# One projection chunk of 512 columns for sparse attention's key and two heads' memory queries

## The chip, the cores and the metric

The kernel runs on one core of a Trainium2 chip. A core has five engines with queues of their own: TensorE (PE, with its weight loads shown apart as PEld), VectorE (DVE), ScalarE (ACT), GpSimd (POOL) and SyncE (SP), which here only issues transfers. The metric is the time of one execution on the device in microseconds (us). The time before is the median of three runs.

## What is computed

Two layers of a decoder trunk over 512 tokens of width 1024. In each layer the normed input `h` is projected by one wide matrix `w_in`, whose column groups feed four branches; each branch is lifted back to 1024, gated, summed, and followed by an output projection and a feed-forward part. The change touches two of these column groups:

```python
h = rmsnorm(x, norm_mix)
(a_x, a_b, a_c, d_q, d_k, d_v, i_q, i_k, i_w,
 g_q, g_f, g_i, g_g, m_q, gate_logits) = split_cols(h @ w_in)
...
k = partial_rope(rmsnorm(d_k.reshape(b, s, 1, 64), dsa_k_norm), cos, sin)[:, :, 0]
...
mq = rmsnorm(m_q.reshape(b, s, 4, 128), mem_q_norm)
ml = jnp.einsum('bshd,bmhd->bhsm', mq, mk) * (128 ** -0.5)
mp = jax.nn.softmax(ml, axis=-1)
y_m = jnp.einsum('bhsm,bmhd->bshd', mp, mv)
```

The first is the key chunk of the sparse attention, 256 columns: key (64), value (64) and the first two of eight index heads (128). The second is the query of the memory attention, four heads of 128 columns, each normed over its own 128 columns, against 256 memory tokens.

## The kernel before

**Layout.** `h` is held feature-major: 8 chunks of 128 features, each 128 partitions x 512 tokens, split into a high and a low part of type fp32r. Every product is three matmuls, high x high, high x low, low x high (`mm3`, lines 316, 317 and 319, where nearly all matmuls of the profile have their line). The norm of `h` is not applied to `h` itself: its reciprocal `r_t` (one number a token, tokens on the partitions) or `r_b` (the same as a row, copied to all partitions) is multiplied in when a product is read out of PSUM.

**Weight chunks.** `wchunk` loads a column group of a weight matrix in parts of 128 x 1024 numbers (tiles `w_raw`, four buffers, issued by SyncE, line 220), and splits each part: ScalarE makes `w_hi` (line 101, the helper for all activations), VectorE `w_lo` (line 245), three buffers each. A 256-column group over 8 feature chunks is two parts of four chunks; a 512-column group is four parts of two.

**Two ways to use a chunk.** `features` makes a feature-major product: the weights are the stationary operand, 512 tokens of `h` move through, one PSUM bank for 128 columns. `tokens` and `tokens_wide` make a token-major one: 128 tokens of `h` are stationary and the weight columns move, so a matmul is as wide as the column group, and there are four products, one for each tile of 128 tokens. `tokens_wide` goes through the parts in the outer loop and needs all four banks at once; with `in_turn` a part's matmuls wait in order for the part before.

**PSUM.** Eight banks of 128 x 512: three `mm` (projections), three `tr` (transposes, norm sums, and a fourth bank for wide products), two `at` (attention).

**The stages around the change.** In `mixer`, four generators run in turn by a script of letters, `EARLY`: `m` is the memory attention (`mem_branch`), `b` the sparse attention's projections, `c` the short convolution, `s` the selection of keys, `n` the late fetch of `r_b`. Each letter runs a generator to its next `yield`; the order so written is the priority by which a planner, with a simulated timeline, orders each engine's queue. Parts inside `tc.high_priority` go ahead of it; `add_manual_dep` fixes an order of two instructions by hand.

**Memory queries before.** For heads 0 and 1 (`q == 0`) and for 2 and 3, `mem_branch` loads a 256-column chunk, makes two feature-major products with `features`, and reads each product out three times: scaled into `qg_hi`, squared into `sq`, and the remainder into `qg_lo` (line 759). The head's mean square per token comes from TensorE: four matmuls with a column of 1/128 (line 762), then `r2`, the reciprocal root, and a factor `mrs`. After a `yield`, each half of 256 tokens of a head is one step: dots into an `at` bank, maximum (line 781), exponentials, scaling, transposes (line 798), product with the values.

**Keys before.** `projections` starts with the 256-column key chunk: for each token tile 24 matmuls with `tokens`, then `key_out` copies the bank into `vt` and `wide` (three copies, all scaled by `r_t`), and `key_heads` does norm, rotation, two transposes (`turn_heads`, line 929) and the copies into the attention's operands. Then come the index chunk of 456 columns and the query chunk of 512, both with `tokens_wide`.

**Fixed orders near it.** In layer 0 the row `r_b` is copied out of a `gate` buffer on ScalarE behind the fourth exponential of the memory attention; the first conv product is read out with `r_b` (line 709). In layer 1, `r_t` comes from four matmuls (line 378) and a short chain on ScalarE and VectorE, and `r_b` by a write and a read of DRAM (lines 367 and 369). Layer 1's mixer follows on `add_down`, whose products leave their `mm` banks by line 1253.

Of the kernel before, what the change touches and what calls it, by code (L numbers as in the profile page):

```python
# [15 lines left out]
U8 = mybir.dt.uint8  # L16
# [5 lines left out]
P = 128  # L22
# [23 lines left out]
EARLY = ["mnmbmcmcbmmmsccbmscmbscmbsbbss", "mnmbmcmcbmmmsccbmscmbscmbsbbss"]  # L46
# [27 lines left out]
def hybrid_trunk(ctx: ExitStack, tc: tile.TileContext, x, x_t, mem, mem_t, positions, columns, w_in,  # L74
# [44 lines left out]
    consts.tile([P, 320], U8, name="spacer")  # L119
# [90 lines left out]
    class Chunk:  # L210
        def __init__(self, src, kt, n):
            self.kt, self.step = kt, min(kt, 1024 // n)
            self.parts = []
            for k in range(0, kt, self.step):
# [4 lines left out]
                if len(src.shape) == 2:  # L219
                    made = [nc.sync.dma_start(raw[:, i - k:j - k], src[i * P:j * P].rearrange("(k p) n -> p k n", p=P))  # L220
                            for i, j in (((k, k + 1), (k + 1, e)) if not raw_loads else ((k, e),))]
                    loaded[0] = made[-1]
                    raw_loads.append(loaded[0])
                    at = len(raw_loads)
                    if at < 4:
                        for i in made:
                            tc.add_manual_dep(i.ins, mem_loads[at - 1].ins.name, order, reason="operands first")
                    if at < 3:
                        tc.add_manual_dep(mem_loads[at].ins, loaded[0].ins.name, order, reason="weights first")
                    if keys:  # L230
                        tc.add_manual_dep(loaded[0].ins, keys.pop().ins.name, order, reason="keys first")
                else:
                    for g in range(2):
                        nc.sync.dma_start(raw.rearrange("p k (g c) -> p k g c", g=2)[:, :, g, :], src[:, k:e, g, :])
# [385 lines left out]
    def mixer(l, h, norms, cm):  # L620
# [79 lines left out]
        scaled = []  # L700
# [35 lines left out]
        def mem_branch(mp, y_m):  # L736
            r2 = small(NT, "r2", 1)
            dve.tensor_mul(r2, r_t, r_t)
            for q in range(2):
                w = wchunk(w_in[l][:, C_MQ + q * 256:C_MQ + (q + 1) * 256], KD, 256)  # L740
# [8 lines left out]
                pqs = features(w, h, (0, 1))  # L749
                for j, pq in enumerate(pqs):  # L750
                    qh = mp.tile([P, S], F32R, name="qg_hi", bufs=2)
                    ql = mp.tile([P, S], F32R, name="qg_lo", bufs=2)
                    sq = scratch512(S)
                    with tc.high_priority(offset=AHEAD):
                        i = A(qh, pq, AF.Copy, scale=col(74 + l))
                        if l == 0 and q == 0 and j == 0:
                            after_two.append(i)
                        A(sq, pq, AF.Square)
                        dve.scalar_tensor_tensor(ql, pq, col(74 + l), f(qh), op0=OP.mult, op1=OP.subtract)
                    pm = tr_ps()  # L760
                    for t in range(NT):
                        pe.matmul(pm[:, t:t + 1], sq[:, t * P:(t + 1) * P], ones_h[:, 0:1], start=True, stop=True)
                    ms, rs = small(NT), small(NT, "mrs", 3)
                    dve.tensor_mul(ms, pm[:, :NT], r2)
# [57 lines left out]
        with pool_("dsa") as dp:  # L822
# [69 lines left out]
            with pool_("idx") as ip:  # L892
# [53 lines left out]
                def key_out(ps, t):  # L946
                    u = wide()[:, :4 * HD]
                    with tc.high_priority(offset=AHEAD):
                        A(vt[:, t, :], ps[:, HD:2 * HD], AF.Copy, scale=r_t[:, t:t + 1])
                        A(u[:, HD:2 * HD], ps[:, 0:HD], AF.Copy, scale=r_t[:, t:t + 1])  # L950
                        A(u[:, 2 * HD:], ps[:, 2 * HD:4 * HD], AF.Copy, scale=r_t[:, t:t + 1])
                    return u

                def key_heads(u, t):
                    w = by_head(u)
# [57 lines left out]
                def projections():  # L1013
                    w = wchunk(w_in[l][:, C_DK:C_DK + 256], KD, 256)
                    for t in range(NT):
                        ps = mm_ps()[:, :256]
                        tokens(w, h, t, ps)
                        key_heads(key_out(ps, t), t)
# [11 lines left out]

                y_m, y_a = new_y(), new_y()
# [680 lines left out]
```

## Time and profile before

| | |
|---|---|
| median of three runs | 1957.95 us (1957.91 to 1958.73) |
| the profiled execution | 1957.13 us, of which 1955.4 are its span |
| VectorE, ScalarE busy | 74%, 60% of the span |
| layer 0's mixer starts, layer 1's mixer starts | 54.3 us, 1003.8 us |

A line of the timeline has the start in us, the length in us, the engine, the line of the kernel, the operation, the tiles written and read, the shape, and how many like instructions were merged. Matmuls overlap: the next starts before the one before has ended, so lengths can't be added up, and the price of a matmul in the queue is the distance from one start to the next. A matmul of type f32 (transposes excepted) leaves two records. A windows line gives a stretch's length and each engine's busy time with its number of instructions. In a waits line the engine named first stood idle for the total, the times and the longest given; in the groups by form, the numbers behind the bar are busy us and the mean ns of one.

### The profile page before, as it was taken

The page shows a single profiled execution, that of the slowest core. Times are in us where ns is not written, and L with a number is a line of the kernel's source. Part 1 is how long each engine was busy: PE and PEld are TensorE (multiplying, and loading weights), DVE is VectorE, ACT ScalarE, POOL GpSimd, SP SyncE. Part 2 cuts the span into 40 slices and gives each one's busy share as a digit, 9 for nine tenths or more (in the row PEclk, how much of TensorE's full clock was granted, in tenths as well). Part 3 has the DMA queues.
Part 4 walks back from the last instruction along what each step waited for, and adds up shares of the span by engine and source line. Part 5 has one row for each costly group of instructions (what it writes and reads, how often), then busy time and mean ns, then how long its engine had stood idle before and what let it go on. Part 6 is the DMA issues. An engine that isn't in the chain of part 4 may idle for free.

```text
span 1955.4 us, 26140 instructions
## 1 busy us (share of the span) xinstructions
PE 1949.9 (100%) x9443; PEld 1618.5 (83%) x9443; DVE 1453.9 (74%) x2552; ACT 1166.1 (60%) x1944; POOL 232.0 (12%) x281
## 2 busy tenths in 40 slices
PE   9999999999999999999999999999999999999999
PEld 7888888878888888888888888888888888888887
DVE  7765899667776776786876688985778667867677
ACT  8654564866764556655644547477667556556464
POOL 1011111111111111110001111111111110111000
PEclk9999999999999999999999999999999999999999
DMA  9576767767777889886687776766667779898864
GB/s 365 189 185 165 178 152 171 159 143 156 178 204 193 240 229 247 248 255 191 200 215 164 180 170 157 170 163 151 153 171 177 207 199 260 240 271 249 238 187 140
DMA packets 221043, 386.79 MB, mean 198 GB/s; under 512 B 13809, under 2 KB 114417, under 8 KB 220657
## 3 DMA queue, kind: packets, MB, share of 16 engines
q1 hardware_dynamic: 162000, 247.69, 40.1%
q0 software_dynamic: 51568, 130.96, 33.2%
q10 hardware_dynamic: 7344, 6.47, 1.0%
q8 instruction: 74, 1.21, 0.3%
q14 instruction: 57, 0.46, 0.1%
HBM read 372.48 MB, written 138.42 MB: 261 GB/s over the span
## 4 chain that ended last, share of the span: by engine, by line
PE 98%; DVE 1%; DMA 0%; ACT 0%; SPq 0%; issue 0%
PE mm L316 24%; PE mm L319 24%; PE mm L317 24%; PE at L316 4%; PE at L317 4%; PE at L319 4%; PE tr L316 2%; PE tr L319 2%; PE tr L317 2%; PE tr L872 1%; PE at L832 1%; PE at L831 1%; PE tr L1592 1%; PE tr L861 1%; PE tr L929 0%; DMA w_raw<-in_mem_w_kv_dram 0%
## 5 line engine op out<-in xcount | busy, mean ns | idle before, releaser
L101 ACT ACTIVATE w_hi<-w_raw 128x1024 fp32r<-128x1024 f32 (+1 forms) x435 | 457.6, 1054 | 367.8 <-PE mm L317 129.1
L316 PE MATMUL mm<-h_hi,w_hi 128*128 128x512 f32 x960 | 378.1, 394 | 0.0
L317 PE MATMUL mm<-h_lo,w_hi 128*128 128x512 f32 x960 | 376.6, 392 | 0.0
L319 PE MATMUL mm<-h_hi,w_lo 128*128 128x512 f32 x960 | 372.8, 394 | 0.0
L1286 DVE TENSOR_TENSOR w_lo<-w_raw,w_hi 128x1024 fp32r<-128x1024 f32 x211 | 256.5, 1219 | 129.9 <-ACT w_hi L101 129.2
L245 DVE TENSOR_TENSOR w_lo<-w_raw,w_hi 128x1024 fp32r<-128x1024 f32 (+1 forms) x224 | 272.7, 1218 | 95.7 <-ACT w_hi L101 95.1
L1301 POOL DMA_DIRECT2D up_sums<-in_ffn_w_up_dram x120 | 121.4, 1012 | 832.0 <-DMA up_sums<-in_ffn_w_up_dram 561.9
L316 PEld LDWEIGHTS mm<-h_hi,w_hi 128*128 128x128 f32 x960 | 180.5, 188 | 36.5 <-DVE zq L1074 0.8
L319 PEld LDWEIGHTS mm<-h_hi,w_lo 128*128 128x128 f32 x960 | 180.2, 188 | 36.1 <-DVE w_lo L245 0.5
L317 PEld LDWEIGHTS mm<-h_lo,w_hi 128*128 128x128 f32 x960 | 180.5, 188 | 35.3
L319 PE MATMUL mm<-w_hi,h_lo 128*128 128x512 f32 (+2 forms) x408 | 151.7, 373 | 0.0
L317 PE MATMUL mm<-w_lo,h_hi 128*128 128x512 f32 (+2 forms) x408 | 151.7, 372 | 0.0
L316 PE MATMUL mm<-w_hi,h_hi 128*128 128x512 f32 (+2 forms) x408 | 145.6, 372 | 0.0
L1301 POOL DMA_DIRECT2D w_sums<-in_ffn_w_down_dram x66 | 62.3, 944 | 327.1 <-DMA w_sums<-in_ffn_w_down_dram 193.8
L316 PEld LDWEIGHTS mm<-w_hi,h_hi 128*128 128x128 f32 x408 | 76.8, 188 | 12.2 <-ACT w_hi L101 0.2
L317 PEld LDWEIGHTS mm<-w_lo,h_hi 128*128 128x128 f32 x408 | 76.9, 188 | 12.1
L319 PEld LDWEIGHTS mm<-w_hi,h_lo 128*128 128x128 f32 x408 | 76.9, 188 | 11.7
L319 PE MATMUL mm<-y_hi,w_lo 128*128 128x512 f32 x192 | 75.7, 394 | 0.0
L317 PE MATMUL mm<-y_lo,w_hi 128*128 128x512 f32 x192 | 75.3, 392 | 0.0
L316 PE MATMUL mm<-y_hi,w_hi 128*128 128x512 f32 x192 | 75.1, 393 | 0.0
L101 ACT ACTIVATE prob<-prob,small 128x128 f32<-128x128 f32 (+3 forms) x128 | 68.9, 553 | 10.3 <-DVE small L847 6.2
L317 PE MATMUL mm<-w_lo,a_hi 128*128 128x512 f32 (+1 forms) x163 | 64.0, 393 | 0.0
(462 smaller groups left out, 4193.2 us busy)
## 6 DMA issues: line engine op xcount, KB each, us to landing
w_raw<-in_w_in_dram SPq DMA_DIRECT2D x140, 512.0 KB, 4.7
up_sums<-in_ffn_w_up_dram POOLq DMA_DIRECT2D x120, 512.0 KB, 6.9
w_raw<-up_sums SPq DMA_DIRECT2D x80, 512.0 KB, 5.3
w_raw<-in_ffn_w_up_dram SPq DMA_DIRECT2D x60, 512.0 KB, 5.0
w_sums<-in_ffn_w_down_dram POOLq DMA_DIRECT2D x54, 512.0 KB, 6.6
up_sums<-up_sums POOLq DMA_DIRECT2D x40, 512.0 KB, 5.2
w_raw<-in_w_lift_dram SPq DMA_DIRECT2D x32, 512.0 KB, 4.7
w_raw<-in_ffn_w_down_dram SPq DMA_DIRECT2D x24, 512.0 KB, 5.1
```

Source lines behind the costliest of these rows:

```text
L101: i = act.activation(dst, src, func, **kw)
L245: i2 = dve.tensor_sub(lo, raw, f(hi))
L316: made += [pe.matmul(ps, ah, bh, start=first, stop=False, skip_group_check=more), pe.matmul(ps, ah, bl, start=False, stop=False, skip_grou ...
L317: pe.matmul(ps, ah, bl, start=False, stop=False, skip_group_check=more)]
L319: made += [pe.matmul(ps, al, bh, start=False, stop=last, skip_group_check=more)]
L831: return [pe.matmul(ps, q[:, hh, s], k[0][:, :n], start=True, stop=False), pe.matmul(ps, q[:, hh, s], k[1][:, :n], start=False, stop=True)]
L832: pe.matmul(ps, q[:, hh, s], k[1][:, :n], start=False, stop=True)]
L861: turn = pe.transpose(pp[:, (2 * e + i) * P:(2 * e + i + 1) * P], probs[2 * i + e][:, b * P:(b + 1) * P], ident)
L872: i = pe.matmul(pv[e * HD:(e + 1) * HD, c], vt[:, b, :], pt[:, b, e * 2 * P:(e + 1) * 2 * P], start=b == 0, stop=b == t)
L1286: two = A(hi, raw, AF.Copy), dve.tensor_sub(lo, raw, f(hi))
L1301: i = nc.gpsimd.dma_start(dst, src, **kw)
L1592: turns.extend(pe.transpose(ps[:, t * P:(t + 1) * P], us[t][:, j * P:(j + 1) * P], ident) for t in range(NT))
```

## The change

The key chunk (256 columns) and the queries of memory heads 0 and 1 (256 columns) become one chunk of 512 columns, loaded by two transfers a part, and used token-major by `tokens_wide` into three `mm` banks and one `tr`. `key_out` copies the second half of each bank unscaled beside the first, squares it on ScalarE with a scale that makes the sum a mean, and sums it on VectorE into `mean_sq`. In `mem_branch`, for `q == 0`, the four tiles are turned by eight transposes into two `tr` banks, and from there the high and low parts are made as before; the norm takes `mean_sq` in place of the matmuls. Heads 2 and 3 stay as they were. `key_heads` moves into a step of its own; the script has one `b` more, `b` first, and the first conv step ahead of the first attention step. An order by hand on the first copy of the queries falls away, and an unused tile shrinks by the size of `mean_sq`.

```diff
-EARLY = ["mnmbmcmcbmmmsccbmscmbscmbsbbss", "mnmbmcmcbmmmsccbmscmbscmbsbbss"]
+EARLY = ["bnmbcmmcmbmmmsccbmscmbscmbsbbss", "bnmbcmmcmbmmmsccbmscmbscmbsbbss"]
...
-                if len(src.shape) == 2:
+                if isinstance(src, tuple):
+                    for g in range(2):
+                        nc.sync.dma_start(raw.rearrange("p k (g c) -> p k g c", g=2)[:, :, g, :],
+                                          src[g][k * P:e * P].rearrange("(k p) n -> p k n", p=P))
+                elif len(src.shape) == 2:
...
-                w = wchunk(w_in[l][:, C_MQ + q * 256:C_MQ + (q + 1) * 256], KD, 256)
+                if q:
+                    w = wchunk(w_in[l][:, C_MQ + q * 256:C_MQ + (q + 1) * 256], KD, 256)
...
-                pqs = features(w, h, (0, 1))
+                if q:
+                    pqs = features(w, h, (0, 1))
+                else:
+                    pqs = [tr_ps() for _ in range(2)]
+                    for j, pq in enumerate(pqs):
+                        for t, u in enumerate(first_queries):
+                            pe.transpose(pq[:, t * P:(t + 1) * P], u[:, (2 + j) * P:(3 + j) * P], ident)
...
-                        i = A(qh, pq, AF.Copy, scale=col(74 + l))
-                        if l == 0 and q == 0 and j == 0:
-                            after_two.append(i)
-                        A(sq, pq, AF.Square)
+                        A(qh, pq, AF.Copy, scale=col(74 + l))
+                        if q:
+                            sq = scratch512(S)
+                            A(sq, pq, AF.Square)
                         dve.scalar_tensor_tensor(ql, pq, col(74 + l), f(qh), op0=OP.mult, op1=OP.subtract)
-                    pm = tr_ps()
-                    for t in range(NT):
-                        pe.matmul(pm[:, t:t + 1], sq[:, t * P:(t + 1) * P], ones_h[:, 0:1], start=True, stop=True)
+                    if q:
+                        pm = tr_ps()
+                        for t in range(NT):
+                            pe.matmul(pm[:, t:t + 1], sq[:, t * P:(t + 1) * P], ones_h[:, 0:1], start=True, stop=True)
                     ms, rs = small(NT), small(NT, "mrs", 3)
-                    dve.tensor_mul(ms, pm[:, :NT], r2)
+                    dve.tensor_mul(ms, pm[:, :NT] if q else mean_sq[:, j, :], r2)
...
                 def key_out(ps, t):
-                    u = wide()[:, :4 * HD]
+                    u = wide()
                     with tc.high_priority(offset=AHEAD):
                         A(vt[:, t, :], ps[:, HD:2 * HD], AF.Copy, scale=r_t[:, t:t + 1])
                         A(u[:, HD:2 * HD], ps[:, 0:HD], AF.Copy, scale=r_t[:, t:t + 1])
-                        A(u[:, 2 * HD:], ps[:, 2 * HD:4 * HD], AF.Copy, scale=r_t[:, t:t + 1])
+                        A(u[:, 2 * HD:4 * HD], ps[:, 2 * HD:4 * HD], AF.Copy, scale=r_t[:, t:t + 1])
+                        A(u[:, 4 * HD:], ps[:, 4 * HD:], AF.Copy)
+                    sq = scratch512(S)[:, :2 * P]
+                    A(sq, u[:, 4 * HD:], AF.Square, scale=P ** -0.5)
+                    dve.tensor_reduce(mean_sq[:, :, t], sq.rearrange("p (a b) -> p a b", b=P), axis=AX.X, op=OP.add)
                     return u
...
-                    w = wchunk(w_in[l][:, C_DK:C_DK + 256], KD, 256)
-                    for t in range(NT):
-                        ps = mm_ps()[:, :256]
-                        tokens(w, h, t, ps)
-                        key_heads(key_out(ps, t), t)
+                    w = wchunk((w_in[l][:, C_DK:C_DK + 256], w_in[l][:, C_MQ:C_MQ + 256]), KD, 512)
+                    pss = [mm_ps() for _ in range(MM_BUFS)] + [tr_ps()]
+                    tokens_wide([w], h, KD, pss, in_turn=True)
+                    first_queries.extend(key_out(ps, t) for t, ps in enumerate(pss))
+                    yield
+                    for t, u in enumerate(first_queries):
+                        key_heads(u, t)
                     yield
```

More of the change, by code (lines that the diff above doesn't have):

```diff
@@ L117, in f @@
         return ap.bitcast(F32)
-    consts.tile([P, 320], U8, name="spacer")
+    consts.tile([P, 256], U8, name="spacer")
     ident = consts.tile([P, P], F32, name="ident")
@@ L698, in weave @@
                 pass
-        scaled = []
+        scaled, first_queries, mean_sq = [], [], None
         def conv_branch(y):
@@ L752, in mem_branch @@
                     ql = mp.tile([P, S], F32R, name="qg_lo", bufs=2)
-                    sq = scratch512(S)
                     with tc.high_priority(offset=AHEAD):
-                        i = A(qh, pq, AF.Copy, scale=col(74 + l))
-                        if l == 0 and q == 0 and j == 0:
-                            after_two.append(i)
-                        A(sq, pq, AF.Square)
+                        A(qh, pq, AF.Copy, scale=col(74 + l))
+                        if q:
+                            sq = scratch512(S)
+                            A(sq, pq, AF.Square)
                         dve.scalar_tensor_tensor(ql, pq, col(74 + l), f(qh), op0=OP.mult, op1=OP.subtract)
-                    pm = tr_ps()
-                    for t in range(NT):
-                        pe.matmul(pm[:, t:t + 1], sq[:, t * P:(t + 1) * P], ones_h[:, 0:1], start=True, stop=True)
+                    if q:
+                        pm = tr_ps()
+                        for t in range(NT):
+                            pe.matmul(pm[:, t:t + 1], sq[:, t * P:(t + 1) * P], ones_h[:, 0:1], start=True, stop=True)
                     ms, rs = small(NT), small(NT, "mrs", 3)
-                    dve.tensor_mul(ms, pm[:, :NT], r2)
+                    dve.tensor_mul(ms, pm[:, :NT] if q else mean_sq[:, j, :], r2)
                     rstd_into(rs, ms, small, NT)
@@ L950, in key_out @@
                         A(u[:, HD:2 * HD], ps[:, 0:HD], AF.Copy, scale=r_t[:, t:t + 1])
-                        A(u[:, 2 * HD:], ps[:, 2 * HD:4 * HD], AF.Copy, scale=r_t[:, t:t + 1])
+                        A(u[:, 2 * HD:4 * HD], ps[:, 2 * HD:4 * HD], AF.Copy, scale=r_t[:, t:t + 1])
[3 more added lines that the diff above has]
+                    dve.tensor_reduce(mean_sq[:, :, t], sq.rearrange("p (a b) -> p a b", b=P), axis=AX.X, op=OP.add)
                     return u
                 def key_heads(u, t):
+                    u = u[:, :4 * HD]
                     w = by_head(u)
@@ L1029, in projections @@
                         yield
+                mean_sq = small(2 * NT, "mean_sq", 2).rearrange("p (j t) -> p j t", t=NT)
                 y_m, y_a = new_y(), new_y()
```

## The prediction, made before the run

> **What bounds the kernel now.** I read the page first, then the waits of TensorE, then TensorE's timeline in the two stretches that the change rewrites: 54 to 95 us (layer 0 enters the mixer) and 1003 to 1032 us (layer 1 does).
>
> ```profile
> span 1955.4 us, 26140 instructions
> PE 1949.9 (100%) x9443; PEld 1618.5 (83%) x9443; DVE 1453.9 (74%) x2552; ACT 1166.1 (60%) x1944; POOL 232.0 (12%) x281
> PEclk9999999999999999999999999999999999999999
> PE 98%; DVE 1%; DMA 0%; ACT 0%; SPq 0%; issue 0%
> PE tr L149 <- DVE one L131: 1.2, 1, 1.2
> PE mm L317 <- DVE w_lo L245: 0.4, 1, 0.4
> PE mm L524 <- ACT w_hi L101: 0.4, 1, 0.4
> ```
>
> TensorE is busy for the whole span at the full clock, the chain that ended last lies on it for 98%, and its three waits sum to 2.0 us. So the time is a queue of matmuls, and an instruction taken off that queue shortens the kernel by the distance from its start to the next start, not by its busy time (busy times overlap). An edit on another engine costs nothing until TensorE has to wait for it. The sum below is therefore one of start-to-start distances, plus a search for new waits.
>
> **The matmuls.** Before, a layer's key chunk is 4 token tiles x 8 k x 3 = 96 matmuls of 256 columns, and the first two heads' queries 2 x 8 x 3 = 48 of 512 columns. After, there are 96 of 512 columns. The columns are the same (49,152); only the number of instructions falls, by 48 a layer.
>
> ```profile
> 70.69 0.28 PE L317 MATMUL mm<-w_lo,h_hi 128*128 128x256 f32 x1
> ...
> 76.68 0.29 PE L316 MATMUL mm<-w_hi,h_hi 128*128 128x256 f32 x1
> 76.81 0.60 PE L798 MATMUL tr<-ident,mprob 128*128 128x128 f32 x4
> 77.16 0.36 PE L317 MATMUL mm<-w_lo,h_hi 128*128 128x256 f32 x1
> 77.36 0.28 PE L319 MATMUL mm<-w_hi,h_lo 128*128 128x256 f32 x1
> 83.48 0.39 PE L317 MATMUL mm<-h_lo,w_hi 128*128 128x512 f32 x1
> ...
> 91.21 0.39 PE L319 MATMUL mm<-h_hi,w_lo 128*128 128x512 f32 x1
> ```
>
> From 70.69 to 76.68 are 50 distances between matmuls of 256 columns: 0.120 us each. From 83.48 to 91.21 are 34 between matmuls of 512 columns: 0.227 us. Twice 0.120 is 0.240, so each pair that becomes one matmul saves 0.013 us. A layer: 96 x 0.120 + 48 x 0.227 = 22.4 before, 96 x 0.227 = 21.8 after; saved **0.6 us**.
>
> **The norms.** Before, each head's mean square is four one-column matmuls (L762). After, two heads' norms come from ScalarE squares and VectorE sums, and their queries are turned by 8 transposes into the layout that the dots need.
>
> ```profile
> 67.35 0.95 PE L762 MATMUL tr<-ones_h,sq 128*128 128x1 f32 x8
> 68.16 0.36 PE L317 MATMUL mm<-w_lo,h_hi 128*128 128x256 f32 x1
> 68.36 0.28 PE L319 MATMUL mm<-w_hi,h_lo 128*128 128x256 f32 x1
> ...
> 79.87 0.38 PE L929 MATMUL tr<-ident,wide 128*128 128x128 f32 x2
> 80.01 0.36 PE L319 MATMUL mm<-w_hi,h_lo 128*128 128x256 f32 x1
> 80.21 0.40 PE L316 MATMUL mm<-h_hi,w_hi 128*128 128x512 f32 x1
> L929 PE MATMUL tr<-ident,wide 128*128 128x128 f32 x80 | 12.6, 272 | 0.0
> ```
>
> A head's four norm matmuls (8 records, two a matmul) take 67.35 to 68.16 = 0.81 us, and the matmul behind them is followed after 0.20 us instead of 0.12, so 0.89 in all; two heads, 1.78 us. Two transposes take 79.87 to 80.01 = 0.14, and again the next matmul has 0.08 extra: 0.22, that is 0.11 each. The group of four at 76.81 says the same: 0.35 + 0.08 = 0.43. Eight come to 0.88. A layer saves 1.78 - 0.88 = **0.9 us** here.
>
> **The sum**: 0.6 + 0.9 = 1.5 us a layer, 3.0 for both. Nothing stands on TensorE's idle time, so I pass it through whole.
>
> The by-form row gives a transpose 272 ns, and this is the place where the number can be misread. If that were its price on the queue, eight would cost 2.18 us a layer, more than the norms' 1.78, and the change would win only 0.6 + 1.78 - 2.18 = 0.2 a layer. The Trainium skill (TensorE: Matmul & The Clock Gate, Part 4: PE-mode transpose) states about 275 ns for a transpose in a kernel's context; by it, as an estimate, the total would fall by 0.4 us and not by 3.0. The trace agrees with it for the duration of one (272) and not for the price: starts inside a group are 0.09 to 0.11 us apart, as the rows at 76.81 and 79.87 show.
>
> **What the other engines get.** Each layer ScalarE loses two 512-column squares and gains four 256-column copies and four 256-column squares; VectorE gains four sums of 256 columns.
>
> ```profile
> 66.34 0.59 ACT L101 ACTIVATE sq<-mm 128x512 f32<-128x512 f32 x1
> 80.46 0.31 ACT L101 ACTIVATE vt<-mm,rstd_t 128x64 f32<-128x64 f32 x1
> 80.66 0.57 ACT L101 ACTIVATE wide<-mm,rstd_t 128x64 f32<-128x64 f32 x2
> 82.45 0.38 ACT L101 ACTIVATE y_hi<-at 128x256 fp32r<-128x256 f32 x1
> 45.77 0.69 DVE L536 TENSOR_REDUCE small<-mk_sq_w 128x4 f32<-128x512 f32 x1
> 53.84 27.63 SPq L220 DMA_DIRECT2D w_raw<-in_w_in_dram  x8
> 54.00:80.00 26.00, 25.98 (x176) 23.71 (x175) 18.32 (x68) 16.58 (x43) 3.79 (x8) 1.00 0.74 241
> ```
>
> The copy is like the one at 82.45 (0.38), the square lies between that and the 0.59 at 66.34, the sum below the 0.69 of a 512-column one. That is about +2 us of ScalarE and under +2 of VectorE a layer, where 26 us hold 16.6 and 18.3 of work: covered. The weight splits keep their number (four of 1024 columns). Loads double in number (8 of 256 KB for 4 of 512), in a queue that took 27.6 us over eight of them here, because it waits for free buffers. The mk, mv and row transfers, and the first step of attention, come behind these loads instead of ahead of half of them; the parts of the joint chunk are released one by one, so the next chunk's split can start earlier than behind the old key chunk, which held both parts to its end. From the index projection on, the same work has gone before as before, and I expect that order unchanged. All this I cost at **nothing**. Where the cover could fail is in the waits below.
>
> **Waits that the change adds.** (a) The chunk holds three mm banks and one tr at once. At layer 1's start the third bank is that of the last down projection.
>
> ```profile
> 1003.82 0.39 PE L316 MATMUL mm<-h_hi,w_hi 128*128 128x512 f32 x1
> 1014.39 0.94 PE L378 MATMUL tr<-ones_d,ssq 128*128 128x1 f32 x8
> ...
> 1004.84 0.69 DVE L1253 TENSOR_TENSOR fg<-fg,mm 128x512 f32<-128x512 f32 x1
> 1018.91 0.16 DVE L191 SCALAR_TENSOR_TENSOR rstd_t<-small 128x4 f32<-128x4 f32 x1
> ...
> 54.26 0.48 PE L316 MATMUL mm<-h_hi,w_hi 128*128 128x512 f32 x1
> 88.97 0.56 ACT L101 ACTIVATE mprob<-at,small,mrs 128x256 f32<-128x256 f32 x1
> 89.52 1.12 ACT L101 ACTIVATE rstd<-gate 128x512 f32<-128x512 f32 x1
> 90.72 0.69 DVE L709 TENSOR_TENSOR gate<-mm,rstd 128x512 f32<-128x512 f32 x1
> ```
>
> It is read out by 1005.5; twelve matmuls start the chunk, so it is wanted at 1003.8 + 2.7 = 1006.5. Covered by 1 us.
>
> (b) The copies out of the key chunk need the layer's r_t; the old first step (queries) did not. The first bank is complete at 1003.8 + 78 x 0.227 = 1021.5, r_t stands at 1019.1. Covered by 2 us, and by 5 before the next chunk wants a bank.
>
> (c) Layer 0's row r_b may be copied (89.52) only behind the fourth exp (88.97), and it releases the first conv chunk's banks (90.72). In the new order this chunk stands ahead of both attention halves that hold the four exps. It ends near 54.3 + 21.8 + 10.9 + the 16 transposes = 89; dots, maximum and four exps of 0.55 bring r_b to about 93.5 and the banks to 94. Meanwhile the third bank can take all 24 matmuls of the next chunk's first half (5.4 us), and the attention halves' own 2 us are there. Covered by some 2 us if the order on TensorE uses them; if it doesn't, up to 2 us are lost, in layer 0 alone.
>
> **Forecast.** 1957.95 - 3.0 = **1954.9 us** for the median. In the profiled execution, 0.8 below that median (1957.13, of which 1955.4 span), this is 1954.1. About 0.2%, 3.9 us, is what a measurement of this kernel can tell from no change; the forecast lies inside it.
>
> **Rivals.** 1. The forecast, perhaps with layer 0's first wait (0.4, row of w_lo) going as well: 1954.5 to 1955. Chance 0.50.
> 2. More than the sum: the scheduler's new order also closes small holes that nothing here accounts for, and the time falls below 1954.0. This needs 0.9 us, twice the one wait in the rewritten stretches. 0.22.
> 3. The row r_b opens a hole in layer 0, (c): -3.0 + 2 = 1957. 0.13. For it speaks that the old order had the exps at 88.97 and the row only 1.2 us ahead of its reader; against it, the free third bank.
> 4. Transposes at 0.27 each: 1957.5. 0.05; the rows speak against it.
> 5. Slower: the banks of the joint chunk wait for the norm in layer 1, (b). It decides when the norm's matmuls (1014.39) are put behind the chunk: r_t takes 4.7 us from there (1014.39 to 1019.1), so past 1019 for their start TensorE waits. At the chunk's end, 1025.6, they give r_t at 1030.3, a first bank at 1031.4 (four copies, about 1.1), and TensorE, with the norm's own 0.9 taken off, stands for 5 us: 1959.9, and with case 3's 2 us on top 1961.9 or more. 0.10. Against it: the norm's sum needs no matmul of the chunk, and it was slotted between matmuls of the query chunk before.
>
> The range that holds the time 8 times in 10 goes from 1953.2 (forecast, less that wait, less as much again, less the 0.8 by which runs of one kernel differ here) to 1957.7 (cases 3 and 4): **1953.2 to 1957.7**. Faster by over 0.2% (below 1954.0): 0.22, case 2. Slower by over 0.2% (above 1961.9): 0.06, the worse part of case 5. Within: 0.72.
>
> **What would show it.** In the changed kernel's timeline: 96 matmuls of 512 columns 0.227 us apart in one block of about 21.8 us at each mixer's start; four groups of L762 instead of eight; sixteen transposes of the queries at 0.11 each; the joint chunk's end to the first conv matmul without a gap. Step (a) is wrong if the block's third tile waits; (b) if L378 comes later than 16 us after the block's first matmul; (c) if TensorE has a hole near 92 us. The forecast is wrong as a whole if TensorE's waits grow by more than 1 us, or if the stages behind the index projection come out in another order.

## The result, and the profile after

The changed kernel takes **1977.33 us** (median of 5 runs, 1976.96 to 1979.47) against 1957.91 for the kernel before: ratio 1.0102, 95% interval 1.0087 to 1.0117. It is 19.4 us slower where 3.0 us less were forecast, and it lies far outside the range. The code has moved by some lines: the product's three lines are 320, 321 and 323, a half's transposes 809, the first conv read-out 713, layer 1's norm sums 382.

The page of the changed kernel (span, busy times, granted clock in 40 slices, the chain that ended last by engine), to be held against the same lines of before:

```profile
span 1975.6 us, 25953 instructions
...
PE 1956.2 (99%) x9331; PEld 1617.3 (82%) x9331; DVE 1456.2 (74%) x2560; ACT 1169.0 (59%) x1956; POOL 231.8 (12%) x281
...
PEclk9989999999999999999999999999999999999999
...
PE 94%; DVE 3%; ACT 1%; DMA 1%; issue 1%; SPq 0%; ACTq 0%; DVEq 0%
```

TensorE has 112 records fewer (9331 for 9443) and is busy for longer; 4% of the last chain has gone from it to VectorE, ScalarE and others; and the third slice (99 to 148 us) shows a 8. All waits of TensorE:

```profile
PE tr L809 <- DVE mprob L807: 9.6, 4, 2.6
PE tr L809 <- DVE iqS L950: 2.0, 1, 2.0
PE at L320 <- ACT mpt_hi L101: 1.4, 2, 0.7
PE tr L382 <- DVE ssq L346: 1.3, 1, 1.3
PE tr L149 <- DVE one L131: 1.2, 1, 1.2
PE mm L321 <- DVE w_lo L249: 0.8, 2, 0.5
```

The first four, 14.3 us in all, are new. In the first and the third, the transposes of an attention half, or its product with the values, stand in TensorE's queue before the half's softmax and its copies are done. The second is another thing: the row at 97.29 below shows that transposes which wait 1.96 us were released by VectorE's line 950, the read-out of a `tr` bank by the key heads. They read nothing that this line writes, so what they waited for is a free bank. The fourth is the norm sums of layer 1. The same stretches in the windows view, before and then after (us, busy time and instructions of PE, PEld, DVE, ACT and POOL, granted clock, DMA share, GB/s):

```profile
94.00:105.00 11.00, 11.00 (x59) 9.41 (x58) 6.48 (x14) 4.25 (x11) 2.60 (x3) 1.00 0.61 183
105.00:109.00 4.00, 4.00 (x21) 3.53 (x20) 3.67 (x8) 1.69 (x2) 0.00 (x0) 1.00 1.02 203
```

```profile
94.00:97.00 3.00, 1.33 (x9) 0.80 (x7) 2.75 (x14) 2.38 (x12) 0.00 (x0) 1.00 0.00 0
94.00:105.00 11.00, 6.06 (x30) 4.65 (x29) 7.28 (x25) 5.94 (x20) 0.00 (x0) 0.73 0.09 24
105.00:109.00 4.00, 4.00 (x10) 3.09 (x10) 3.11 (x6) 1.06 (x2) 0.72 (x1) 0.50 0.42 131
...
1018.00:1024.00 6.00, 4.73 (x19) 3.65 (x18) 3.08 (x11) 1.43 (x4) 1.07 (x1) 0.72 1.05 311
...
1068.00:1080.00 12.00, 6.10 (x36) 5.14 (x35) 9.21 (x24) 4.98 (x15) 2.33 (x2) 0.80 0.66 143
```

TensorE idles for 5 us in 94 to 105, then runs at half clock: ten matmuls of 512 columns in 4 us. Over the longer windows neither VectorE nor ScalarE is full: the stalls are mostly chains of dependent work, not a lack of throughput. Only in 94 to 97 us, ahead of the transposes at 97.29, is VectorE busy for 2.75 of 3.00 us, with the key heads' read-outs among others.

For all kernels below I use one measure, the **stall**: over the whole timeline, each matmul's distance to the next start less the distance that its shape has in a full queue (0.227 us for 512 columns, 0.204 for 456, 0.120 for 256, 0.109 a transpose, 0.112 a record of the norms). It holds waits and slower clock. (Over the whole kernel, even before the change, it adds up to some 30 us outside the mixers; how much depends on what one takes for the rare shapes, so of the column "elsewhere" below only the differences count.) By it the kernel before has 1.4 us between 54 and 300 us (layer 0's mixer) and 1.3 between 990 and 1260 (layer 1's); the changed kernel has 13.7 and 13.7. The growth is 24.7 us: 14.3 of waits, and the mean granted clock, 0.995 for 1.000, is worth (1 - 0.995) x 1975.6 = 9.9. Elsewhere the stall is 1.0 us less than before (28.0 for 29.0), and 3.1 us of work are saved: 24.7 - 1.0 - 3.1 = 20.6, for the 20.2 by which the span grew.

**Layer 0**, in the changed kernel's timeline (start, length, engine, line, tiles; in brackets the wait and its releaser):

```profile
88.52 0.28 PE L323 MATMUL at<-mk,qg_lo 128*128 128x256 f32 x1
...
91.91 0.68 DVE L792 TENSOR_REDUCE small<-at 128x2 f32<-128x512 f32 x1
...
97.29 0.66 PE L809 MATMUL tr<-ident,mprob 128*128 128x128 f32 x4 [1.96 <-DVE iqS L950]
98.63 0.39 PE L320 MATMUL at<-mpt_hi,mv 128*128 128x256 f32 x1 [0.69 <-ACT mpt_hi L101]
...
99.78 0.42 PE L323 MATMUL at<-mk,qg_lo 128*128 128x256 f32 x1
...
102.71 1.12 ACT L101 ACTIVATE rstd<-gate 128x512 f32<-128x512 f32 x1
...
103.56 1.09 PE L809 MATMUL tr<-ident,mprob 128*128 128x128 f32 x4 [2.29 <-DVE mprob L807]
...
103.87 1.29 DVE L713 TENSOR_TENSOR gate<-mm,rstd 128x512 f32<-128x512 f32 x2 [0.19 <-ACT rstd L101]
```

The first half's dots end at 88.8, its maximum waits on VectorE behind a weight split and the key heads until 91.91, its transposes for a bank until 97.29, the second half's dots come behind the first half's transposes (99.78), the fourth exponential and so the row `r_b` at 102.71, and the conv banks at 103.87.

**Layer 1** has no such tie to `r_b`, and loses as much:

```profile
1018.79 0.68 DVE L346 TENSOR_TENSOR ssq<-ssq,sq 128x512 f32<-128x512 f32 x1
...
1019.62 1.02 PE L382 MATMUL tr<-ones_d,ssq 128*128 128x1 f32 x8 [1.27 <-DVE ssq L346]
1020.50 0.67 PE L320 MATMUL tr<-w_hi,h_hi 128*128 128x512 f32 x1
...
1069.22 0.28 PE L323 MATMUL at<-mk,qg_lo 128*128 128x256 f32 x1
...
1072.94 0.63 PE L809 MATMUL tr<-ident,mprob 128*128 128x128 f32 x4 [2.62 <-DVE mprob L807]
...
1079.04 0.66 PE L809 MATMUL tr<-ident,mprob 128*128 128x128 f32 x2 [2.54 <-DVE mprob L807]
1079.35 0.73 PE L320 MATMUL tr<-w_hi,h_hi 128*128 128x456 f32 x1
```

Between the second half's dots, which end at 1069.5, and their transposes TensorE has five products of 0.12 us, 0.6 us of work, and the softmax takes longer. In the kernel before, the same half had 13.5 us of other work there, and no wait:

```profile
1033.07 0.28 PE L319 MATMUL at<-mk,qg_lo 128*128 128x256 f32 x1
...
1046.82 0.60 PE L798 MATMUL tr<-ident,mprob 128*128 128x128 f32 x4
```

I call this work the half's cover, and add it up from the timelines with the distances above (us):

| half | before, layers 0 and 1 | changed, layers 0 and 1 |
|---|---|---|
| first | 6.1, 8.6 | 6.3, 14.2 |
| second | 12.6, 13.5 | 0.6, 0.6 |
| third | 7.4, 6.2 | 3.7, 0.6 |
| fourth to eighth | 8.0 to 14.2 | the same, half by half |

So the first half was not squeezed (its wait in layer 0 is the one for a bank), the second and third were, and from the fourth on nothing changed. Two things stand out: directly behind a squeezed pair comes the first matmul into a chunk's *fourth* bank, which is a `tr` bank (1079.35; a part of the third half); and the norm sums (a `tr` bank too) were put ahead of the joint chunk's fourth bank (1020.50), before VectorE had `ssq`.

### The profile page after: what moved, and what is told of

Same layout as the page of the kernel before. It is cut to its first block, busy times and chain, and to the rows that moved or that the text cites. A ratio compares the mean times of both kernels' runs of the same rounds, so it can differ in the third digit from the quotient of the medians.

```text
span 1975.6 us, 25953 instructions
## 1 busy us (share of the span) xinstructions
PE 1956.2 (99%) x9331; PEld 1617.3 (82%) x9331; DVE 1456.2 (74%) x2560; ACT 1169.0 (59%) x1956; POOL 231.8 (12%) x281
## 3 DMA queue, kind: packets, MB, share of 16 engines
q1 hardware_dynamic: 162128, 247.70, 39.8%
## 4 chain that ended last, share of the span: by engine, by line
PE 94%; DVE 3%; ACT 1%; DMA 1%; issue 1%; SPq 0%; ACTq 0%; DVEq 0%
PE mm L320 23%; PE mm L321 23%; PE mm L323 23%; PE at L320 4%; PE at L321 4%; PE at L323 4%; PE tr L320 2%; PE tr L321 2%; PE tr L323 2%; PE tr L883 1%; PE at L843 1%; PE at L842 1%; PE tr L1611 1%; PE tr L872 1%; DVE w_lo L249 1%
## 5 line engine op out<-in xcount | busy, mean ns | idle before, releaser
L320 PE MATMUL mm<-h_hi,w_hi 128*128 128x512 f32 x928 | 367.2, 396 | 0.0
L321 PE MATMUL mm<-h_lo,w_hi 128*128 128x512 f32 x928 | 365.1, 393 | 0.0
L323 PE MATMUL mm<-h_hi,w_lo 128*128 128x512 f32 x928 | 361.5, 395 | 0.0
L320 PEld LDWEIGHTS mm<-h_hi,w_hi 128*128 128x128 f32 x928 | 175.0, 189 | 35.8 <-DVE zq L1093 0.8
L323 PEld LDWEIGHTS mm<-h_hi,w_lo 128*128 128x128 f32 x928 | 174.8, 189 | 35.1 <-issue 0.2
L321 PEld LDWEIGHTS mm<-h_lo,w_hi 128*128 128x128 f32 x928 | 175.1, 189 | 34.0
L321 PE MATMUL mm<-w_lo,h_hi 128*128 128x512 f32 (+1 forms) x392 | 152.4, 389 | 0.2 <-DVE w_lo L249 0.2
L323 PE MATMUL mm<-w_hi,h_lo 128*128 128x512 f32 (+1 forms) x392 | 152.5, 390 | 0.0
L320 PE MATMUL mm<-w_hi,h_hi 128*128 128x512 f32 (+1 forms) x392 | 146.3, 390 | 0.0
L321 PEld LDWEIGHTS mm<-w_lo,h_hi 128*128 128x128 f32 x392 | 73.9, 189 | 14.6 <-DVE w_lo L249 0.7
```

Source lines behind the costliest of these rows:

```text
L320: made += [pe.matmul(ps, ah, bh, start=first, stop=False, skip_group_check=more), pe.matmul(ps, ah, bl, start=False, stop=False, skip_grou ...
L321: pe.matmul(ps, ah, bl, start=False, stop=False, skip_group_check=more)]
L323: made += [pe.matmul(ps, al, bh, start=False, stop=last, skip_group_check=more)]
```

## The experiments

Times in us; the stall as defined above. Where only one run was taken there is no range; e1 to e4, e8, e10 and e12 are such single runs, and a small difference between two of them says little. The kernel before had 1957.5 to 1958.8 (medians) beside these runs.

| kernel | time | stall 54 to 300 | stall 990 to 1260 | elsewhere |
|---|---|---|---|---|
| before | 1957.91 | 1.4 | 1.3 | 29.0 |
| changed | 1977.33 | 13.7 | 13.7 | 28.0 |
| e1_row_early | 1981.89 | 14.6 | 14.0 | 31.3 |
| e2_row_and_script | 1964.22 | 5.9 | 7.7 | 28.7 |
| e3_fourth_bank | 1975.03 | 12.2 | 11.9 | 29.0 |
| e4_before_late_attention | 1975.68 | 9.3 | 12.6 | 28.4 |
| e5_spread | 1962.38 (1961.43 to 1964.02) | 5.6 | 5.8 | 28.5 |
| e6_spread_unmerged | 1969.68 (1969.13 to 1971.35) | 9.5 | 5.8 | 28.1 |
| e7_spread_old_norms | 1977.51 (1976.57 to 1977.77) | 9.7 | 12.4 | 28.7 |
| e8_layer1_spread | 1969.99 | 13.5 | 6.2 | 28.3 |
| e9_heads_later | 1966.52 (1964.52 to 1966.76) | 9.1 | 6.5 | 28.9 |
| e10_heads_later_order_alone | 1969.62 | 9.3 | 9.8 | 28.6 |
| e11_four_banks | 1971.60 (1970.88 to 1972.72) | 5.0 | 4.6 | 39.8 |
| e12_four_banks_late_row | 1976.92 | 11.6 | 4.6 | 38.7 |
| e13_before_four_banks | 1966.44 (1965.30 to 1968.09) | 1.5 | 1.1 | 38.1 |
| e14_four_banks_heads_later | 1970.42 (1969.61 to 1972.18) | 4.2 | 4.7 | 38.7 |
| e15_own_bank | **1953.82** (1953.24 to 1956.09) | 1.5 | 1.4 | 29.0 |
| e16_own_bank_other_order | 1958.91 (1957.92 to 1960.67) | 3.6 | 3.5 | 29.9 |
| e17_before_own_bank | 1957.48 (1956.75 to 1958.92) | 1.4 | 1.2 | 29.1 |

**Row, order or bank.** Theory A: the halves come too late and too close; theory B: layer 0's row is the one cause there; C: the merged chunk loads ScalarE and VectorE so much that what comes next is late; D: `ssq` is late wherever the norm sums stand.

```diff
 e1: on the changed kernel; i is the copy of the second head's queries
+                        if l == 0 and q == 0 and j == 1:
+                            tc.add_manual_dep(row_moves[2].ins, i.ins.name, order, reason="queries first")
...
-                            if len(exps) == 4:
-                                tc.add_manual_dep(row_moves[2].ins, e.ins.name, order, reason="probabilities first")
 e2: e1, and both layers
-"bnmbcmmcmbmmmsccbmscmbscmbsbbss"
+"bnmbcmcbmmmmmsccbmscmbscmbsbbss"
 e3: on the changed kernel, the joint chunk
-                    pss = [mm_ps() for _ in range(MM_BUFS)] + [tr_ps()]
+                    pss = [mm_ps() for _ in range(MM_BUFS)] + [at_ps()]
 e4: on the kernel before, both layers
-"mnmbmcmcbmmmsccbmscmbscmbsbbss"
+"mnbcmmcmbmmmsccbmscmbscmbsbbss"
```

e1: 

> The changed kernel, but in layer 0 the copy of the row r_b stands behind the two copies of the queries instead of behind the fourth exponential. Theory A (two waits in series: the conv banks wait for r_b, and behind them the index chunk's fourth bank waits for three halves of attention): the conv wait goes, the index wait takes its place; layer 0 from the first matmul on h to the first index dots stays within 4 us of the changed kernel's 120.0, total 1973 to 1977. Theory B (r_b is the one cause in layer 0): this stretch falls by 9 to 12 us, total about 1967. Layer 1 unchanged by both.

e2: 

> The changed kernel with the row copy behind the queries' copies, and a script in which one half of attention, not three, stands ahead of the index chunk (and the first conv step, the second conv step and the index follow each other). Theory A (the waits come from the order of steps): layer 0's stretch falls from 120.0 to 107 to 109, layer 1's from 120.0 to about 111, since its wait for the norm's sum stays; total 1955 to 1959. Theory C (the merged chunk loads ScalarE and VectorE so much that whatever comes next is late): the waits move to another place, total above 1968.

e3: 

> The changed kernel, but the joint chunk's fourth bank is taken from the two attention banks instead of the three transpose banks. Theory A: in the changed kernel the norm's four sums (layer 1) had to be put ahead of this bank's first matmul because the transpose banks are handed out in the order written, so TensorE waited 1.4 us for ssq and then ran eight matmuls at half clock; both go, layer 1's stretch falls by 2.5 to 3.5 us, total about 1974. Rival D: ssq is simply late, and the wait or its like stays wherever the sums stand: within 0.7 us of 1977.3. Layer 0 the same by both.

e4: 

> The kernel before, unmerged, with only the script altered: the first conv step ahead of the first two halves of attention, as in the changed kernel. Theory A (order of steps): the waits appear without the merged chunk; layer 0's stretch from 109.2 to 113 to 119, layer 1's less, since the queries are ready 10 us earlier than in the changed kernel; total 1962 to 1972. Theory C: within 2 us of the kernel before.

e1 misses both numbers. The row now stands at 86.36 instead of 102.71, and yet the transposes wait for 12.5 us (four waits, the longest 4.8): without the tie, layer 0 falls into layer 1's order and loses as much. (Some 3.3 of its 4.6 us above the changed kernel lie outside the mixers, nearly all at the weights of the first 54 us, and are not explained.) B, the row as the one cause, has fallen. e4 is the plainest: **without any merging, the order of steps alone** brings 21.9 us of stall, for 2.7. That is more than A expected (1975.68 for 1962 to 1972), and layer 1 loses more than layer 0, not less, but C's "within 2 us" is out. Its waits for `mprob` are nearly those of the changed kernel:

```profile
PE tr L798 <- DVE mprob L796: 9.5, 4, 2.9
```

e3 removes the wait of L382 and the slow matmuls behind it, some 3 us of layer 1's stall, as A had it; 1 us comes back at the halves, and the total is 1975.03 for A's 1974. e2, with one half instead of three ahead of the index chunk, wins 13 us and ends between the two expectations; what stays, beside the norm's sums in layer 1 and 1.4 us at the index dots, is a pair of transposes directly ahead of the query chunk's fourth bank:

```profile
170.86 0.41 PE L809 MATMUL tr<-ident,mprob 128*128 128x128 f32 x2 [1.83 <-DVE mprob L807]
171.03 0.48 PE L320 MATMUL tr<-w_hi,h_hi 128*128 128x512 f32 x1
```

**Spreading the halves.** The next four spread the halves so that each has 7.5 us of work behind its dots; G holds that the joint chunk itself costs the time.

```diff
 e5: e2 and e3, and both layers
+"bnmbcmcbmmmmsccbmmscmbscmbsbbss"
 e6: the kernel before, early row, both layers
+"mnbcmcbmmmmsccbmmscmbscmbsbbss"
 e7: e5, for heads 0 and 1 again, in place of key_out's squares and sums
+                    pm = tr_ps()
+                    for t in range(NT):
+                        pe.matmul(pm[:, t:t + 1], sq[:, t * P:(t + 1) * P], ones_h[:, 0:1], start=True, stop=True)
 e8: the changed kernel, e5's order and e3's bank in layer 1 alone
```

e5: 

> The changed kernel with other steps in the hand-written order (both layers: one attention half ahead of the index chunk, four steps behind it, the fifth half behind the query chunk), layer 0's row behind the copies of the first two queries, the joint chunk's fourth bank from the attention banks. Theory A (a half's transposes stand in TensorE's queue with less matmul work between them and the half's dots than the softmax between takes; in the slower kernel it was 0.6 us for several halves, here it is 7.5 us or more for each by the rows' start-to-start distances): no wait of transposes for mprob over 1 us, and the sum of the prediction comes through, 1954.0 to 1957.0. Theory G (the joint chunk itself, with its fuller banks, eight loads and the extra copies and squares, costs the time): waits stay, above 1960.

e6: 

> The kernel before (key chunk and queries separate, norms by TensorE) with the same spread of the halves and the early row. A: the time of before, 1957 to 1959, and 3.0 us (2.3 to 3.7) above e5_spread, which is then the worth of the joint chunk and the sums alone. G: at or below e5_spread.

e7: 

> e5_spread with the first two heads' norms again by squares of 512 columns on ScalarE and 8 one-column matmuls on TensorE a layer, in place of the 256-column squares and VectorE sums. A, by the 0.89 us a head of the prediction: 4 heads, 3.6 us above e5_spread (2.8 to 4.4). If the norms' matmuls hide behind something on TensorE: within 0.7.

e8: 

> The changed kernel with the spread order and the attention bank in layer 1 alone, layer 0 as in the changed kernel. A: the 11.7 us of TensorE's stall of layer 1 go and layer 0's stay: 1965 to 1967. If the layers lean on each other: above 1970 or below 1962.

In e5 no transpose waits for `mprob` any more, as A had it, but some 4 us a layer have moved to where the last half now stands, at 249 and 1201 us, so the time is not A's but lies in G's "above 1960". e6 shows that the joint chunk isn't needed for that: the same order is a bad one for the kernel before as well (stall 15.3). Both numbers of e6 missed: it stands 7.3 us above e5, 3.1 of work and 3.9 of stall. e7 has 32 records more than e5 (9363 for 9331), which at 0.112 us are the 3.6 us of theory A; the other 11.5 are nearly all stall (10.7 in the table), since two more `tr` banks are asked for (`PE tr <- DVE iqS`, 4.9 us). So the price of the sums fits the count of records; the time doesn't confirm it. e8, at 1969.99, lies between its two expectations: layer 0 keeps its stall (13.5) and layer 1 has e5's (6.2), so the layers don't lean on each other, but layer 1 didn't lose all.

**Key heads behind the first half.** The same mends with an order in which the last halves stand where they stood before:

```diff
 e9: e5's row and bank; e10: the changed kernel; both layers
+"bnmmbcmcbmmmmsccbmscmbscmbsbbss"
```

e9: 

> The joint chunk kept, with the early row and the fourth bank from the attention banks, and another order of steps in both layers: the first attention half ahead of the key heads, the second half between the key heads and the index chunk, then four steps behind the index chunk and the rest as in the changed kernel, so that the last halves stand where they stood in the kernel before. By the rows' distances the halves' transposes have 7.5 us or more of TensorE work behind their dots, but the second half's first pair, which has 3.5 to 3.9. Theory A (the cover of each half decides): no wait of transposes over 1 us but at that pair, TensorE's stall within 2 us of the kernel before: 1954 to 1957. Rival (some stall moves to another place whatever the order is, 4 us a layer as in the two spread kernels): 1961 to 1964.

e10: 

> The changed kernel with that order of steps alone: layer 0's row behind the fourth exp and the fourth bank from the transposes' ring as in the changed kernel. A: layer 1 is as in e9_heads_later but for the norm's sums (about 3.2 us), and layer 0 has the second half's pair with 1.3 us of cover and the row behind it: 8 to 14 us above e9_heads_later. If order alone was the cause and row and bank do nothing: within 2.

Both numbers missed: 1966.5 (ratio to before 1.0041, 1.0027 to 1.0055) is above the rival's 1961 to 1964 too, though the rival's kind is there, stall that moves to another place. e10 is 3.1 us above e9, neither 8 to 14 nor within 2: in this order row and bank do nothing in layer 0 (9.3 and 9.1), and layer 1's 3.3 fit the norm's sums, whose wait of 1.3 us at L382 e10 has and e9 has not. In e9's timeline, TensorE breaks off in the middle of the index chunk:

```profile
106.71 0.37 PE L323 MATMUL mm<-w_hi,h_lo 128*128 128x456 f32 x1
109.53 0.46 PE L940 MATMUL tr<-ident,wide 128*128 128x128 f32 x2 [2.44 <-DVE wide L974]
112.65 0.66 PE L809 MATMUL tr<-ident,mprob 128*128 128x128 f32 x2 [2.66 <-DVE mprob L807]
112.96 0.73 PE L320 MATMUL tr<-w_hi,h_hi 128*128 128x456 f32 x1
```

The key heads' transposes (109.53) and the second half's (112.65) both wait, and again the fourth bank comes right behind the latter. This gave **theory B of the later runs**: the `tr` banks are a ring handed out in the order in which the program asks. A half that is written ahead of a chunk must have its transposes done before the chunk's fourth bank can be had; and as the chunk goes part by part, that bank is wanted after 18 matmuls of its first part, not at its end.

**Parting the ring.**

```diff
 e11: the changed kernel with the early row; e12: without it; e13: the kernel before; e14: e11 in e9's order
-MM_BUFS = 3
-TR_BUFS = 3
+MM_BUFS = 4
+TR_BUFS = 2
...
-pss = [mm_ps() for _ in range(MM_BUFS)] + [tr_ps()]
+pss = [mm_ps() for _ in range(MM_BUFS)]
 (wherever a chunk of tokens takes its banks, the value chunks included)
```

e11: 

> The changed kernel with its own order of steps, the early row, and the eight banks shared out otherwise: four matmul banks and two transposes' banks in place of three and three, so that no chunk of tokens takes its fourth bank from the ring of the transposes. Theory B (the fourth bank of the joint, index and query chunks stands in a ring that is handed out in program order, so a half that is written ahead of a chunk must have its transposes done before that chunk's first part can end; that pulls them right behind their dots): every half has 6.3 us or more of TensorE work behind its dots in this order, waits of transposes for mprob fall below 1 us, and the time is 1954 to 1957. Rival H (the joint chunk makes the softmax and the key heads late, and no hand-out of banks helps: about 4 us a layer stay somewhere): 1961 to 1966.

e12: 

> As e11_four_banks, with layer 0's row behind the fourth exp as in the changed kernel. The row's tie then costs in layer 0 alone: 3 to 8 us above e11_four_banks. If the ring was all: within 1.

e13: 

> The kernel before with four matmul banks and two transposes' banks, nothing else. B: it had no stall to lose: within 1.5 us of 1957.7, so that what e11_four_banks gains over it is the joint chunk's work alone, 2.3 to 4 us. Two banks too few for the transposes: above 1960.

e14: 

> e11_four_banks with the order of steps of e9_heads_later. B: 1954 to 1957, within 2 us of e11_four_banks. H: 1961 to 1966.

The times of e11, e13 and e14 are outside B's, those of e11 and e14 above H's too, and e13 lies where two banks were to be too few (above 1960). The profile says why. e14 has e9's order of steps; its timeline:

```profile
102.60 0.28 PE L323 MATMUL at<-mk,qg_lo 128*128 128x256 f32 x1
...
116.60 0.60 PE L809 MATMUL tr<-ident,mprob 128*128 128x128 f32 x4
```

The second half's transposes stand 14 us behind their dots, in the middle of the index chunk, without a wait, and no wait for `mprob` is left in e11 or e14. So the ring was what pulled them forward. The cleanest pair is e1 and e11, which have the same order and the same early row and differ in the banks alone: 12.5 us of waits for `mprob` become none, and the stall of the two mixers falls from 28.6 to 9.6. In layer 0 it takes both, the row and the banks: 13.7 with neither, 14.6 with the early row, 11.6 with the banks parted (e12), 5.0 with both. In layer 1, which has no tie to the row, the banks alone bring 4.6. The rest of e11's waits, the longest three:

```profile
PE mm L320 <- ACT w_hi L101: 5.1, 5, 1.2
PE at L842 <- ACT wide L101: 2.5, 5, 1.0
PE tr L872 <- ACT pt L101: 1.4, 2, 0.7
```

Four and two banks are a bad share elsewhere: the first and the last row, and some 9 us more stall outside the mixer's first part, in e13 as well, where nothing else was changed. (Whether two `tr` banks or four `mm` banks are to blame was not parted.) The second row is at the index dots. e12 prices the row's tie once the ring is out of the way: 5.3 us, all in layer 0.

**A bank of its own.**

```diff
 e15, e16: the joint chunk, early row; e17: the kernel before
-TR_BUFS = 3
+TR_BUFS = 2
...
     def tr_ps():
+        turn[0] += 1
+        if not mixing[0] and turn[0] % 3 == 0:
+            return fourth_ps()
         return pat.tile([P, 512], F32, name="tr", bufs=TR_BUFS)
+    def fourth_ps():
+        return pat.tile([P, 512], F32, name="fourth", bufs=1)
...
 in projections: fourth_ps() for tr_ps(); mixing[0] is True while the script runs
 e15: "bnmmbcmcmbmmscmcbmscmbscmbsbbss", e16: "bnmmbcmcmbmmmsccbmscmbscmbsbbss"
```

e15: 

> The joint chunk with a bank of its own for every fourth tile of a chunk while the mixer's first part runs (three matmul banks, two transposes' banks, one fourth bank; elsewhere the three go round for the transposes as before), the early row, and an order of steps with the first half ahead of the key heads, three halves ahead of the index chunk and none between the query chunk's neighbours: by the rows' distances every half has 7.7 us or more of TensorE work behind its dots, the index dots start where they did before, and the last half stands where it stood before. B: no wait of transposes for mprob, no new wait of 1 us elsewhere: 1954 to 1957, faster than the kernel before by about 3.4 us. H: some 4 us a layer remain, 1961 to 1966.

e16: 

> As e15_own_bank with three steps of attention between the index and the query chunk instead of two: the fifth half comes 18 us earlier and the index dots 17 us later. In the four-bank kernels late index dots came with a stall of about 2.5 us a layer on the copies of the scores: B with that stall, 1957 to 1961; without it, within 1 us of e15_own_bank.

e17: 

> The kernel before with the bank of its own, its own order of steps. B: no stall to lose, within 1.5 us of 1957.6.

e15 takes 1953.82 us, **faster than both kernels**: ratio to before 0.9982, 0.9973 to 0.9991 (11 runs); B's range is missed by 0.2 us at its lower end. Every half has a cover of 7.7 us or more, the second 13.7 and 14.1. Its page and all of TensorE's waits:

```profile
span 1952.2 us, 25930 instructions
...
PE 1946.2 (100%) x9331; PEld 1610.4 (82%) x9331; DVE 1457.7 (75%) x2560; ACT 1168.3 (60%) x1956; POOL 232.0 (12%) x281
```

```profile
PE tr L157 <- DVE one L139: 1.2, 1, 1.2
PE mm L536 <- ACT w_hi L101: 0.8, 2, 0.6
PE mm L329 <- DVE w_lo L257: 0.7, 2, 0.5
```

These are the three waits of the kernel before (the lines have moved), 2.7 us in all for 2.0, and the stall is that kernel's too. The bank alone does nothing: e17's ratio to before is 1.0000 (0.9991 to 1.0009). And a good order is still needed: e16 has the same banks, all halves covered, and loses 2.1 us a layer, most of it at the index dots, its time inside what was expected of B with that stall.

## Why the prediction was wrong

- **The sum of TensorE's work: right.** The joint chunk's matmuls are 0.227 apart, the turned queries cost what the other transposes cost, sixteen records of norm matmuls a layer are left of 32. Where no stall hides it, that is e15 against e17: 1957.48 - 1953.82 = 3.7 us for a forecast of 3.0, which the scatter of the runs can't tell apart. By the records' own distances it is 3.1: 96 pairs at 0.013 make 1.25, 32 norm records at 0.112 are 3.58, less 16 transposes at 0.109, 1.74. (The range's lower end, by its own terms, is 1953.3 and not 1953.2; nothing hangs on it.)
- **Transposes at 0.27 (rival 4): rightly set aside.** In the changed kernel's timeline a pair goes from 76.03 to the next matmul at 76.17, 0.07 each, and 0.08 are added behind it: 0.11 each, as predicted. The Trainium skill (TensorE: Matmul & The Clock Gate, Part 4: PE-mode transpose) puts a transpose in a kernel's context at about 275 ns. The length of one agrees with that, 272 ns here; its price in the queue doesn't.

```profile
76.03 0.38 PE L760 MATMUL tr<-ident,wide 128*128 128x128 f32 x2
76.17 0.48 PE L320 MATMUL mm<-h_hi,w_hi 128*128 128x512 f32 x1
```

- **"Covered" for ScalarE and VectorE's extra work: right in throughput.** e15 has that work with no more stall than the kernel before.
- **"From the index projection on ... I expect that order unchanged. All this I cost at nothing": the step that failed.** The cover was asked for in loads and busy engines and at the three places (a) to (c), and not in TensorE work between a half's dots and its transposes. From the fourth half on the order did stay. Ahead of it, the first dots move in layer 0 from 67.11 to 87.93, behind the joint chunk and a conv chunk, while three halves are still written ahead of the index chunk; the ring, and in layer 0 the row, then set the second half's transposes 0.6 us of work behind their dots, where 12.6 and 13.5 stood before, and the third half's 3.7 and 0.6, for 7.4 and 6.2. A term put at nothing so became most of 14.3 us of waits and 24.7 us of stall. e4 (the order without the merging) and e1 against e11 (the banks parted, the order kept) show the two parts of the cause.
- **(a), the third bank: right**, no tile of the joint chunk waits for `mm`.
- **(b), r_t in layer 1: wrong in sign.** I feared sums behind the chunk; they came too early. L382 stands 5.5 us behind the chunk's first matmul, ahead of its fourth bank, and waits for `ssq`: 1.3 us of wait, some 3 of stall with the slower clock. A fourth bank from another ring takes it away (e3: no such wait).
- **(c), r_b in layer 0: right in kind, wrong in size.** Instead of 93.5 the row stands at 102.71 (the first half's maximum behind the key heads, the second half's dots behind the first half's transposes). The cover named, 24 matmuls into the third bank, was used (88.64 to 94.37). "Up to 2 us, in layer 0 alone" became 12.3 us of stall there, but that is not the row's alone: moving only the row mends nothing (e1), and with the ring out of the way it is worth 5.3 us (e12).
- **Rival 5, slower:** right side, wrong mechanism. No rival had the ring, though the kernel's description names all its users: transposes, norm sums, and a fourth bank for wide products.

Open: e15's order was not run with the three shared `tr` banks, nor the changed kernel's order with e15's banks, so how much of e15's gain over the changed kernel is the order's and how much the bank's isn't parted; that the banks matter is shown in two other orders (e1 against e11, e9 against e14), where the products got a fourth bank as well. Why the index dots lose some 2 us a layer in e11, e14 and e16 was seen only as a wait for ScalarE's copies of the scores. The early weight waits of e1 are not explained. And whether the norm's sums could be held back by hand behind the joint chunk's first part was not tried.

## What to carry to other kernels

When a change moves a step on the bounding engine, list for each later step with a producer and a consumer on that engine how much of its own work stands between the two, before and after; where that falls below the latency of the chain between, price the difference, for every such step. And look for buffers of one ring that serve steps of unlike lifetime: a ring handed out in program order ties them together, and a new order turns that tie into a queue order. A gain of 3 us in work was real here, but it came out only in a kernel that had both a bank of its own for the fourth tile and an order fitted to it.

## What the runs showed of the hardware

**The clock fell after short waits.** In the changed kernel, behind waits of 1.96 and 0.69 us, the products of 256 columns start 0.21 us apart from 99.14 on, for 0.12 before; after a third wait, of 2.29 us, the granted clock in 105 to 109 us is 0.50 and 512-column matmuls start 0.43 us apart. Behind a single wait of 1.27 us (1018 to 1024) it is 0.72 on average. The Trainium skill (TensorE: Matmul & The Clock Gate, Part 1: The HAM clock gate) puts the drop after an idle window of about 3.4 us, in a window that runs free of the kernel. In the changed kernel no single wait is that long (the longest is 2.6 us); e1 has one of 4.8, and behind it, in 116 to 124 us, the granted clock is 0.50. Nor does the wait's length decide alone: in e7, 104 to 112 us hold 3.16 us of idle, in waits of 2.46 and 0.69, at clock 1.00:

```profile
104.00:112.00 8.00, 4.84 (x28) 3.91 (x27) 7.69 (x17) 3.56 (x11) 1.15 (x1) 1.00 0.78 150
```

So a wait of TensorE cost here from little more than its own length (e7) to over twice as much (some 3 us of stall for the 1.27), and in the changed kernel's mixers, on average, 1.7 times as much: 24.7 us more stall for 14.3 of waits. What decides it the traces don't show.
